# A half tile times its norm weight, made by ACT in place of DVE

## The chip, the cores and the metric

The kernel runs on one core of a Trainium2 chip. Five engines matter: PE (TensorE, the matrix products), DVE (VectorE), ACT (ScalarE), POOL (GpSimd, used here almost only to issue transfers) and SP (SyncE, which issues the other transfers). Each engine works through its own list of instructions in order and meets the others only at semaphores. The metric is the time of one execution in microseconds; the figure for the kernel before is the median of three runs, 1158.26 us.

## The reference

A small decoder trunk: 512 tokens, width 1024, two layers. The first mixes by a gated delta rule, the second by sliding-window attention; both also attend to 256 memory tokens. Behind the mixing, each layer has a gated feed forward of width 2816. Cut to what matters here:

```python
def swiglu(h, w_gate_up, w_down):
    gu = h @ w_gate_up
    return (jax.nn.silu(gu[..., :D_FF]) * gu[..., D_FF:]) @ w_down

for layer in range(DEPTH):
    ...
    x = x + concatenate([mix_out, mem_o], -1) @ w_out[layer]
    x = x + swiglu(rms_norm(x, ln_ffn[layer]), w_gate_up[layer], w_down[layer])
```

`rms_norm(x, g)` divides each token by its root mean square and multiplies each of the 1024 features by its weight g.

## The kernel before, in words

Activations stand with features on the 128 partitions and the 512 tokens along the free axis, so x is eight tiles of 128x512. The root mean square is divided out after the products (`rstd`); what goes into them is h = x times g. Every fp32 operand is split in two: a rounded high part, written by ACT (`copy`, line 138: an activation of kind Copy, with an optional scale per partition), and the rest, written by DVE. A product is then three matmuls: high by high, high by low, low by high (`mm3`). `weight` (line 181) splits a loaded weight tile in this way into whi and wlo; `split_gain` (line 171) does the same for x times g.

**The output projection** (`output`, line 933) runs over eight rows m. When PE has finished row m, DVE adds it to the residual x[m] (the last of these additions is kept as `self.ended`), ACT makes the high part of h[m], DVE the low part l, ACT squares x[m] (sq) and DVE adds the square to a running sum (sqa). One matmul with ones over that sum gives `rstd`.

**The feed forward** (`ffn`, line 966) begins with gate 0 and up 0, then gates 1 and 2, all as plain products of 512 tokens. From then on gate and up columns are made in pairs by `quarters` (line 1109), which splits weights and tokens in halves and forms seven products of half size in place of eight, as Strassen's scheme does. A pair adds weight halves on DVE and on POOL's queue (accumulating transfers into the ws tiles), splits each sum, and copies intermediate results out of PSUM on ACT (the fs tiles) before PE adds the next product onto the same bank.

**The token sums** (`token_sums`, line 1082) are the other operand of these products: combinations of the two token halves of x[j] and x[j + 4], each times its weight. There are four of them per layer (j = 0 to 3), each made once and used by all later products. For one j, the code makes

- c: the second half of x[j] times its weight, 128x256 (one buffer, so the next j must wait for its readers)
- t0: the first half of x[j] times its weight, less c; t1 from t0 and x[j + 4]; t2: the second half of x[j + 4] times its weight, less c; t3 from t1. All four are quarters of one tile, raw
- the split of raw into two T tiles, high on ACT and low on DVE

c is read by t0 and t2.

**What sets the order.** The program is traced in the order of the code; a planner then puts each engine's instructions into a list of its own, by its own estimates of when each can start, in which instructions from later in the code may move up into gaps. It places the token sums among the last rows of the output projection, gate 0 and up 0. Where its choice is not wanted, the code adds an edge without a semaphore (`nosync`) that keeps two instructions of one engine in order. In the second layer such an edge keeps c of j = 1 to 3 behind `self.ended`, the last residual addition.

Of the kernel before, what the change touches and what calls it, by code (L numbers as in the profile page):

```python
# [13 lines left out]
ALU = mybir.AluOpType  # L14
# [71 lines left out]
class Builder:  # L86
# [995 lines left out]
    def token_sums(self, fp, layer, j, h):  # L1082


        nc, q = self.nc, T // 2
        if j == 0:
            self.minus = self.t(fp, [P, 4], F32, "minus")
            self.ts(self.minus, self.gains[:, G_FFN[layer] + 4:G_FFN[layer] + 8], -1.0, ALU.mult)
        g0, g1 = (self.gain(G_FFN[layer], j + i) for i in (0, 4))
        n1 = self.minus[:, j:j + 1]  # L1090
        x0, x1 = self.x[j], self.x[j + 4]
        c = self.t(fp, [P, q], F32, "fc")
        raw = self.t(fp, [P, D], F32, "raw")
        t = [raw[:, i * q:(i + 1) * q] for i in range(4)]
        ins = nc.vector.tensor_scalar(out=c, in0=x0[:, q:], scalar1=g0, scalar2=None, op0=ALU.mult).ins
        if layer and j:

            self.nosync(ins, self.ended)
        self.stt(t[0], x0[:, :q], g0, c, ALU.mult, ALU.subtract)
        self.stt(t[1], x1[:, q:], n1, t[0], ALU.mult, ALU.subtract)  # L1100
        self.stt(t[2], x1[:, q:], g1, c, ALU.mult, ALU.subtract)
        self.stt(t[3], x1[:, :q], n1, t[1], ALU.mult, ALU.subtract)
        hl = self.weight(None, raw=raw, pool=fp, tags=("T", "T"), bufs=8)
        parts = {f"t{i + 1}": [x[:, i * q:(i + 1) * q] for x in hl] for i in range(4)}
        parts["11"] = [x[:, :q] for x in h[j]]
        parts["21"], parts["22"] = ([x[:, i * q:(i + 1) * q] for x in h[j + 4]] for i in range(2))
        return parts
# [304 lines left out]
```

## Time and profile before

| what | value |
|---|---|
| median of three runs | 1158.26 us (1158.03 to 1158.34) |
| the profiled execution's own time | 1158.37 us |
| its span, first to last instruction | 1156.6 us |
| busy: PE, DVE, ACT | 1138.6, 834.8, 627.3 us |
| the changed line, L1095: instructions, median | 8, 0.346 us |
| where it runs | 308.2 us (first layer) to 812.9 us (second layer) |

In the lists below, a row gives the start in us from the span's start, the length in us, the engine, the line of the kernel, the operation, and what it writes and reads with partitions x elements; x2 at the end means two in a row, whose length is their sum. In brackets stands the time the engine was idle before it, and what ended that. Lengths include a tail in which the next instruction has already begun, so the step from start to start is what an instruction takes from a full list. Lines of waits read: engine, tile and line that waited, who was waited for: us in total, times, longest.

### The profile page before, as it was taken

The page shows a single profiled execution, that of the slowest core. Times are in us where ns is not written, and L with a number is a line of the kernel's source. Part 1 is how long each engine was busy: PE and PEld are TensorE (multiplying, and loading weights), DVE is VectorE, ACT ScalarE, POOL GpSimd, SP SyncE. Part 2 cuts the span into 40 slices and gives each one's busy share as a digit, 9 for nine tenths or more (in the row PEclk, how much of TensorE's full clock was granted, in tenths as well). Part 3 has the DMA queues.
Part 4 walks back from the last instruction along what each step waited for, and adds up shares of the span by engine and source line. Part 5 has one row for each costly group of instructions (what it writes and reads, how often), then busy time and mean ns, then how long its engine had stood idle before and what let it go on. Part 6 is the DMA issues. An engine that isn't in the chain of part 4 may idle for free.

```text
span 1156.6 us, 19275 instructions
## 1 busy us (share of the span) xinstructions
PE 1138.6 (98%) x7330; PEld 995.3 (86%) x7330; DVE 834.8 (72%) x1559; ACT 627.3 (54%) x1251; POOL 85.1 (7%) x97
## 2 busy tenths in 40 slices
PE   7999999999999999999999999999999999999996
PEld 7788777877899998899998877788899988999986
DVE  5674886767888877488965777839988644889554
ACT  6489572366566642256653554856666412666433
POOL 0220000000101101011100000001011000111000
PEclk9999999999999999999999999999999999999999
DMA  8243441225657736367623421116577633676232
GB/s 311 85 150 110 135 120 65 91 92 164 183 130 176 177 103 167 114 168 178 161 84 97 124 73 40 53 55 197 130 177 188 155 92 111 169 188 151 78 98 84
DMA packets 72559, 151.20 MB, mean 131 GB/s; under 512 B 16732, under 2 KB 18932, under 8 KB 72468
## 3 DMA queue, kind: packets, MB, share of 16 engines
q1 hardware_dynamic: 61332, 129.54, 35.8%
q0 software_dynamic: 11136, 20.45, 11.1%
q8 instruction: 57, 0.93, 0.3%
q14 instruction: 34, 0.28, 0.1%
HBM read 143.00 MB, written 6.96 MB: 130 GB/s over the span
## 4 chain that ended last, share of the span: by engine, by line
PE 93%; DVE 4%; ACT 1%; DMA 1%; issue 0%; DVEq 0%; SPq 0%; ACTq 0%
PE pj L145 43%; PE g L145 38%; PE sc L145 6%; PE qk L145 3%; PE pt L145 2%; PE pt L149 1%; DVE wlo L152 1%; ACT sm L133 1%; DVE qv L155 1%; DVE big L152 0%; PE g L149 0%; DVE kn L155 0%; DVE btmp L152 0%; DMA wraw<-in_win 0%; DMA mem<-in_memT 0%
## 5 line engine op out<-in xcount | busy, mean ns | idle before, releaser
L139 ACT ACTIVATE whi<-wraw 128x512 fp32r<-128x512 f32 (+3 forms) x324 | 241.0, 750 | 254.6 <-PE pj L145 155.1
L152 DVE TENSOR_TENSOR wlo<-wraw,whi 128x512 fp32r<-128x512 f32 (+3 forms) x324 | 271.2, 846 | 100.5 <-ACT whi L139 94.3
L145 PE MATMUL pj<-h,whi 128*128 128x512 f32 (+1 forms) x652 | 257.4, 396 | 0.0
L145 PE MATMUL pj<-l,whi 128*128 128x512 f32 (+1 forms) x652 | 255.0, 392 | 0.0
L145 PE MATMUL pj<-h,wlo 128*128 128x512 f32 (+1 forms) x652 | 254.2, 391 | 0.0
L145 PE MATMUL g<-T,whi 128*128 128x256 f32 x1216 | 220.6, 282 | 0.9 <-ACT fs L139 0.9
L145 PEld LDWEIGHTS g<-T,whi 128*128 128x128 f32 x1216 | 187.0, 189 | 2.2 <-DVE fu L155 1.1
L145 PE MATMUL g<-T,wlo 128*128 128x256 f32 x608 | 171.1, 281 | 0.0
L145 PEld LDWEIGHTS pj<-h,whi 128*128 128x128 f32 x652 | 122.5, 188 | 28.6 <-issue 3.6
L145 PE MATMUL g<-h,whi 128*128 128x256 f32 (+1 forms) x500 | 146.6, 293 | 0.0
L145 PE MATMUL g<-h,wlo 128*128 128x256 f32 (+1 forms) x500 | 145.8, 292 | 0.0
L145 PE MATMUL g<-l,whi 128*128 128x256 f32 (+1 forms) x500 | 145.5, 291 | 0.0
L145 PEld LDWEIGHTS pj<-l,whi 128*128 128x128 f32 x652 | 122.6, 188 | 25.3 <-issue 1.1
L145 PEld LDWEIGHTS pj<-h,wlo 128*128 128x128 f32 x652 | 122.6, 188 | 25.3 <-issue 0.6
L145 PEld LDWEIGHTS g<-T,wlo 128*128 128x128 f32 x608 | 114.4, 188 | 0.0
L145 PEld LDWEIGHTS g<-h,whi 128*128 128x128 f32 x500 | 95.0, 190 | 2.3 <-issue 0.5
L145 PEld LDWEIGHTS g<-l,whi 128*128 128x128 f32 x500 | 94.9, 190 | 2.3 <-issue 0.5
L145 PEld LDWEIGHTS g<-h,wlo 128*128 128x128 f32 x500 | 95.0, 190 | 1.7
L1120 POOL DMA_DIRECT2D ws<-in_wgu x38 | 33.6, 884 | 722.7 <-ACT h L139 231.8
L139 ACT ACTIVATE whi<-ws 128x512 fp32r<-128x512 f32 x76 | 47.9, 631 | 49.2 <-PE g L145 41.4
L152 DVE TENSOR_TENSOR fu<-pj,rstd 128x512 f32<-128x512 f32 (+1 forms) x34 | 22.4, 659 | 54.4 <-PE pj L145 54.4
L152 DVE TENSOR_TENSOR wlo<-ws,whi 128x512 fp32r<-128x512 f32 x76 | 52.0, 685 | 7.5 <-ACT whi L139 7.3
(379 smaller groups left out, 1695.2 us busy)
## 6 DMA issues: line engine op xcount, KB each, us to landing
wraw<-in_wgu SPq DMA_DIRECT2D x50, 512.0 KB, 4.3
ws<-in_wgu SPq DMA_DIRECT2D x76, 256.0 KB, 3.6
ws<-in_wgu POOLq DMA_DIRECT2D x76, 256.0 KB, 4.8
wraw<-in_win SPq DMA_DIRECT2D x26, 512.0 KB, 3.5
wraw<-in_wdn SPq DMA_DIRECT2D x32, 384.0 KB, 3.1
wraw<-in_wdn SPq DMA_DIRECT2D x32, 320.0 KB, 2.9
wraw<-in_wgu SPq DMA_DIRECT2D x38, 256.0 KB, 4.3
wraw<-in_wout SPq DMA_DIRECT2D x16, 512.0 KB, 3.6
```

Of the source, the lines that this page charges most:

```text
L133: ins = self.nc.scalar.activation(out, in_, func, **kw).ins
L139: self.copied = self.nc.scalar.activation(out, in_, AF.Copy, **kw).ins
L145: return self.nc.tensor.matmul(out, lhsT, rhs, start=start, stop=stop, skip_group_check=more).ins
L149: return self.nc.tensor.transpose(out, in_, self.ident[:k, :k]).ins
L152: return eng.tensor_tensor(out=out, in0=a, in1=b, op=op).ins
L155: return self.nc.vector.scalar_tensor_tensor(out=out, in0=in0, scalar=scalar, in1=in1, op0=op0, op1=op1).ins
L1120: nc.gpsimd.dma_start(s1, a22, accum_op=ALU.add)
```

## The change

c is made by ACT's scaled copy in place of DVE's multiplication. The edge behind `self.ended`, which was put on c, is now put on t0, the next instruction of DVE.

```diff
         t = [raw[:, i * q:(i + 1) * q] for i in range(4)]
-        ins = nc.vector.tensor_scalar(out=c, in0=x0[:, q:], scalar1=g0, scalar2=None, op0=ALU.mult).ins
+        self.copy(c, x0[:, q:], scale=g0)
+        ins = self.stt(t[0], x0[:, :q], g0, c, ALU.mult, ALU.subtract)
         if layer and j:
 
             self.nosync(ins, self.ended)
-        self.stt(t[0], x0[:, :q], g0, c, ALU.mult, ALU.subtract)
         self.stt(t[1], x1[:, q:], n1, t[0], ALU.mult, ALU.subtract)
```

## The prediction

> **What bounds the kernel now.** I read the totals first, then the busy time by stretch, then who makes PE wait, and only then the lists of the three engines around the two places where the changed line runs.
>
> ```profile
> PE 1138.6 (98%) x7330; PEld 995.3 (86%) x7330; DVE 834.8 (72%) x1559; ACT 627.3 (54%) x1251; POOL 85.1 (7%) x97
> ...
> PE 93%; DVE 4%; ACT 1%; DMA 1%; issue 0%; DVEq 0%; SPq 0%; ACTq 0%
> ...
> L1095 DVE TENSOR_SCALAR fc<-x,gains x8: 344/346/349, 308.2 to 812.9; 128x256 f32<-128x256 f32 x8
> ...
> 308.00:334.00 26.00, 26.00 (x119) 21.36 (x119) 23.95 (x43) 14.93 (x21) 3.50 (x4) 1.00 0.65 168
> 812.00:826.00 14.00, 13.12 (x72) 11.24 (x71) 13.54 (x25) 8.92 (x16) 0.86 (x1) 1.00 0.24 58
> ...
> 660.00:788.00 128.00, 127.93 (x797) 99.98 (x796) 88.02 (x257) 79.77 (x222) 0.00 (x0) 1.00 0.21 67
> ```
>
> PE sets the time. In a stretch row the figures after the length are busy us of PE, PEld, DVE, ACT and POOL. In the first layer's token sums (308 to 334) PE has no gap; in the second layer's it misses 0.88 us between 812 and 826, where DVE is busy 13.54 of 14 us and ACT 8.92. The changed line runs eight times, four in each place. What PE waited for between 300 and 826, and what DVE waited for between 788 and 826:
>
> ```profile
> PE g L145 <- ACT fs L139: 0.9, 1, 0.9
> ...
> DVE l L155 <- ACT h L139: 2.0, 1, 2.0
> DVE wlo L152 <- ACT whi L139: 0.4, 2, 0.3
> ```
>
> So one wait, for one ACT instruction, is all that PE loses near the change. Its history, from the lists of ACT, DVE and PE (start, length):
>
> ```profile
> 822.20 0.69 DVE L152 TENSOR_TENSOR wraw<-wraw 128x512 f32<-128x512 f32 x1
> 822.98 0.63 ACT L139 ACTIVATE whi<-wraw 128x512 fp32r<-128x512 f32 x1 [1.84 <-DVE wraw L152]
> ...
> 824.56 0.61 ACT L139 ACTIVATE whi<-wraw 128x512 fp32r<-128x512 f32 x1
> 825.08 0.36 ACT L139 ACTIVATE fs<-g 128x256 f32<-128x256 f32 x1
> 825.49 0.50 PE L145 MATMUL g<-T,whi 128*128 128x256 f32 x2 [0.88 <-ACT fs L139]
> ```
>
> ACT stood idle 1.84 us for DVE's add of two weight halves, then ran without a gap (two more instructions between the rows shown), and fs is the fifth; PE may add the next product to that bank only when fs has copied it. DVE's lateness at 822.20 is therefore paid by PE, one for one, up to 0.88 us.
>
> **The change, part by part.** Removed from DVE: eight multiplications. Added to ACT: eight scaled copies of the same half tile. New waits: DVE's first product of a token sum (t0) waits for ACT; and, as the tile c has one buffer, ACT's next c waits for DVE's third product (t2) of the sum before. No transfer is added or moved, so the SP queue keeps its list; POOL's queue, which waits for readers of the ws buffers, can only see DVE readers a little earlier.
>
> What leaves DVE is the step from the start of c to the start of the next instruction:
>
> ```profile
> 798.24 0.34 DVE L1095 TENSOR_SCALAR fc<-x,gains 128x256 f32<-128x256 f32 x1
> 798.62 0.48 DVE L155 SCALAR_TENSOR_TENSOR raw<-x,gains,fc 128x256 f32<-128x256 f32 x1
> 799.02 0.68 DVE L152 TENSOR_TENSOR x<-pj,x 128x512 f32<-128x512 f32 x1
> ...
> 802.87 0.75 DVE L155 SCALAR_TENSOR_TENSOR l<-x,gains,h 128x512 fp32r<-128x512 f32 x1 [1.98 <-ACT h L139]
> 803.53 0.69 DVE L152 TENSOR_TENSOR sqa<-sqa,sq 128x512 f32<-128x512 f32 x1
> ...
> 805.48 0.35 DVE L1095 TENSOR_SCALAR fc<-x,gains 128x256 f32<-128x256 f32 x1
> 805.74 1.22 DVE L152 TENSOR_TENSOR wlo<-wraw,whi 128x1024 fp32r<-128x1024 f32 x1
> ...
> 811.67 0.87 DVE L155 SCALAR_TENSOR_TENSOR raw<-x,gains,fc 128x256 f32<-128x256 f32 x2
> ...
> 812.86 0.35 DVE L1095 TENSOR_SCALAR fc<-x,gains 128x256 f32<-128x256 f32 x1
> 813.12 0.48 DVE L155 SCALAR_TENSOR_TENSOR raw<-x,minus,raw 128x256 f32<-128x256 f32 x1
> ...
> 816.47 0.88 DVE L155 SCALAR_TENSOR_TENSOR raw<-x,gains,fc 128x256 f32<-128x256 f32 x2
> ```
>
> In the second layer the first c (0.38 us of step) lies ahead of DVE's 1.98 us wait for h: it frees nothing, that wait just grows. The three later ones (first and last shown) step 0.26 us each, and behind 802.87 DVE waits only the 0.4 us of the row above. So 3 x 0.26 = 0.78 us goes from a full list, the add at 822.20 starts at 821.42, fs ends 0.78 earlier, and of PE's 0.88 us some 0.1 is left: **-0.78 us**. Late next is PE's own arrival.
>
> What ACT gets, by the nearest rows (the same shape and scale operand, at the end of the kernel), and the places where it can lie:
>
> ```profile
> L139 ACT ACTIVATE T<-x,gains x12: 494/495/497, 1131.2 to 1136.1; 128x256 f32<-128x256 f32 x12
> ...
> 1132.12 4.49 ACT L139 ACTIVATE T<-x,gains 128x256 f32<-128x256 f32 x11
> ...
> 796.52 0.61 ACT L142 ACTIVATE sq<-x 128x512 f32<-128x512 f32 x1
> 801.16 1.06 ACT L139 ACTIVATE whi<-wraw 128x1024 fp32r<-128x1024 f32 x1 [4.03 <-DMA wraw<-in_wgu]
> 802.13 0.71 ACT L139 ACTIVATE h<-x,gains 128x512 fp32r<-128x512 f32 x1
> ...
> 808.84 1.06 ACT L139 ACTIVATE T<-raw 128x1024 fp32r<-128x1024 f32 x1 [2.71 <-DVE raw L155]
> 818.77 1.06 ACT L139 ACTIVATE T<-raw 128x1024 fp32r<-128x1024 f32 x1 [2.01 <-DVE raw L155]
> ```
>
> One takes 0.495 us, and in a row 4.49 / 11 = 0.41. ACT's gaps of 4.03, 2.71, 2.01 and 1.84 us hold one each, and c's input was complete rows earlier, so I cost the copies at nothing on the path. If that cover is missing, a copy pushes what stands behind it by 0.41. Where exactly the planner places them no row shows. Bounds: from below the whole 0.88 of PE's wait goes (-0.88); from above the copy lands behind the whi that waits 4.03 us, which is the third rival. I take -0.78, since c(0) fits in the 4.03 gap and a later c has time: both readers of the third c (the pair at 811.67) are done by 812.54, and the fourth is first read at 816.47, 3.9 us on.
>
> First layer: DVE there has room, and PE does not wait.
>
> ```profile
> 332.93 0.69 DVE L152 TENSOR_TENSOR fg<-pj,rstd 128x512 f32<-128x512 f32 x1 [1.33 <-PE pj L145]
> ```
>
> DVE catches up with PE and idles 1.33 us before the products begin, so 0.26 us less, four times, makes that idle longer: **0**. The moved ordering edge costs nothing by itself: it keeps t0 of the later sums behind the last residual add, as it kept c.
>
> Sum: -0.78 us. The profiled execution took 1158.37 us in all (span 1156.6, 1.77 around it), so 1157.59 on its own base; that execution lies 0.11 above the median of 1158.26, so 1157.5 as a median. A change within 0.2% (2.3 us, 1155.9 to 1160.6) is about what a measurement of this kernel cannot tell from none.
>
> **The rivals.** First, *nothing moves*: something else ends fs late, for instance a different ACT order in front of it. Then 1158.3. For it: fs already stands behind four ACT instructions it does not need. Against: all four are back to back, and the one idle ahead of them is put down to DVE.
>
> Second, *the hand-over is exposed*: t0 waits for a copy that ACT begins only when t0 is next. DVE then pays 0.495 plus the 0.03 between the end of h (802.13 + 0.71) and l at 802.87, less the 0.26 saved, three times: +0.8, which fs and PE follow: 1159.1. Against: those 3.9 us. [...]
>
> Third, on the other side, *c(0) behind a waiting weight*: the planner lists ACT's c(0) after the whi that waits (for a transfer in the second layer, for PE in the first), and keeps t0 ahead of the last residual add x on DVE. It has already put that whi ahead of an h that was ready sooner. The rows for the first layer and for PE:
>
> ```profile
> 310.03 0.47 DVE L155 SCALAR_TENSOR_TENSOR raw<-x,minus,raw 128x256 f32<-128x256 f32 x1
> 310.43 0.68 DVE L152 TENSOR_TENSOR x<-g,x 128x512 f32<-128x512 f32 x1
> 314.14 0.69 DVE L152 TENSOR_TENSOR sqa<-sqa,sq 128x512 f32<-128x512 f32 x1
> ...
> 310.10 1.06 ACT L139 ACTIVATE whi<-wraw 128x1024 fp32r<-128x1024 f32 x1 [3.29 <-issue]
> 311.07 1.05 ACT L139 ACTIVATE T<-raw 128x1024 fp32r<-128x1024 f32 x1
> ...
> 315.53 1.02 PE L145 MATMUL g<-sqa,consts 128*128 128x512 f32 x2
> ...
> 804.28 1.12 PE L145 MATMUL g<-sqa,consts 128*128 128x512 f32 x2
> ```
>
> Second layer: c(0) at 802.13 to 802.63, t0 one step of 0.4 us, x at 803.06 to 803.75, h 0.71 more, l at 804.46 against 802.87: 1.6 later with one product ahead of x, 2.8 with four. PE's sum of squares (804.28) has 0.06 us to spare behind sqa, so PE is 1.5 to 2.7 late there; fs is late by that less the 0.78 saved: +0.7 to +1.9. First layer: c(0) ends at 311.56 behind whi, and x moves from 310.43 to 312.0 (one product ahead) or 313.2 (four), 1.6 or 2.8 late; sqa has 0.7 to spare (314.83 against 315.53): +0.9 to +2.1. In today's lists one product stands ahead of x in the second layer and four in the first, which gives 0.7 + 2.1 = +2.8 and 1161.1; the ends are 1159.9 and 1162.3. It decides as slower from both layers together on. Against: ACT is idle 4.03 and 3.29 us before these two whi, with c's input ready.
>
> *Faster by over 0.2%* would need 2.3 us of PE waits, and there are 0.88 around the change; the 128 us of attention behind the first layer hold 0.07. Only a reordering elsewhere would do it.
>
> **How the numbers follow.** The forecast 1157.5 has 0.46, with a range of its own of 1157.2 to 1158.0; nothing moves 0.09; exposed hand-over 0.12; the waiting weight 0.26, of which 0.03 stays under 1160.6; faster by a reordering 0.07. So within 0.2%: 0.46 + 0.09 + 0.12 + 0.03 = 0.70; slower 0.23; faster 0.07. The range runs from 1157.0 (all of PE's wait gone, and 0.2 of spread) to 1161.8, most of the third rival; left out are the faster case and that rival's upper end.
>
> **What would show it.** Right: c rows on ACT of about 0.495 us, c(0) ahead of the whi near 801; DVE's list from l to wraw 0.78 us shorter; PE's wait for fs at 0.1 us; no new PE wait near 315 and 804. Wrong: DVE rows t0 released by ACT c, an x add later than 799 or 310.4 against PE's rows, or PE waiting for h, l or sqa. A PE or transfer list in another order than before, far from the two places, would break the argument altogether.

## The result, and the profile after

The changed kernel takes 1160.53 us in the median (1159.02 to 1164.06) against 1158.28 us before (1157.39 to 1158.87) in the same comparison: a ratio of 1.0021, interval 1.0013 to 1.0028. It is slower by 2.25 us, where 0.8 us less had been forecast. The profiled execution took 1159.56 us with a span of 1157.8, which is 1.19 us over the profiled execution of before; the rest of the difference of the medians is the subject of the last section. One execution of the kernel before (2891.29 us) and one of the changed kernel (1732.60 us) are far off all others and are left out of every figure.

In the first layer nothing is lost. Between 788 and 840 us, around the token sums of the second layer, PE loses 1.11 us more than before (51.12 less 50.01). The busy time by stretch, first of the kernel after, then of the kernel before (after the length stand PE, PEld, DVE, ACT and POOL, then the granted clock):

```profile
308.00:334.00 26.00, 26.00 (x122) 21.48 (x121) 23.19 (x38) 16.71 (x25) 3.50 (x4) 1.00 0.61 163
...
788.00:840.00 52.00, 50.01 (x281) 43.01 (x280) 45.24 (x75) 32.44 (x53) 6.93 (x8) 1.00 0.58 157
```

```profile
788.00:840.00 52.00, 51.12 (x293) 44.54 (x292) 47.93 (x81) 31.85 (x51) 6.94 (x8) 1.00 0.60 163
```

In place of one wait PE now has three, and DVE waits longer and for other things. What PE waited for between 280 and 840 us, and DVE between 785 and 835, in the kernel after:

```profile
PE g L145 <- ACT fs L139: 1.0, 1, 1.0
PE g L145 <- DVE T L152: 0.6, 1, 0.6
PE pj L145 <- DVE l L155: 0.4, 1, 0.4
...
DVE T L152 <- ACT T L139: 3.3, 2, 2.2
DVE wlo L152 <- ACT whi L139: 2.8, 3, 2.3
```

The lists of PE, SP and POOL are the same as before, instruction by instruction. Those of DVE and ACT are not: in the first layer some T moved, and in the second the planner put the lists together anew. DVE's list after, from the low part of gate 1's weight on:

```profile
801.82 1.23 DVE L152 TENSOR_TENSOR wlo<-wraw,whi 128x1024 fp32r<-128x1024 f32 x1 [2.33 <-ACT whi L139]
802.97 0.75 DVE L155 SCALAR_TENSOR_TENSOR l<-x,gains,h 128x512 fp32r<-128x512 f32 x1
...
805.83 1.23 DVE L152 TENSOR_TENSOR T<-raw,T 128x1024 fp32r<-128x1024 f32 x1 [1.12 <-ACT T L139]
...
812.75 1.23 DVE L152 TENSOR_TENSOR T<-raw,T 128x1024 fp32r<-128x1024 f32 x1 [2.20 <-ACT T L139]
...
823.14 0.69 DVE L152 TENSOR_TENSOR wraw<-wraw 128x512 f32<-128x512 f32 x1
823.75 1.22 DVE L152 TENSOR_TENSOR T<-raw,T 128x1024 fp32r<-128x1024 f32 x1
```

ACT's list after:

```profile
800.73 1.06 ACT L139 ACTIVATE whi<-wraw 128x1024 fp32r<-128x1024 f32 x1 [4.23 <-DMA wraw<-in_wgu]
801.69 0.49 ACT L139 ACTIVATE fc<-x,gains 128x256 f32<-128x256 f32 x1
802.09 0.71 ACT L139 ACTIVATE h<-x,gains 128x512 fp32r<-128x512 f32 x1
...
808.07 0.51 ACT L139 ACTIVATE fc<-x,gains 128x256 f32<-128x256 f32 x1 [1.32 <-DVE raw L155]
808.49 0.67 ACT L133 ACTIVATE rstd<-g,eps 128x512 f32<-128x512 f32 x1
809.19 0.63 ACT L133 ACTIVATE rstd<-rstd 128x512 f32<-128x512 f32 x1
809.84 1.28 ACT L124 ACT_TABLE_LOAD   x1
811.13 0.63 ACT L133 ACTIVATE fg<-fg 128x512 f32<-128x512 f32 x1
811.67 1.04 ACT L139 ACTIVATE T<-raw 128x1024 fp32r<-128x1024 f32 x1
```

Three things are new in them. The low part wlo of gate 1's weight, which needs a transfer and ACT's whi, stands ahead of l of the last row; before, it stood 2.87 us behind l (805.74 against 802.87). On ACT, T of the second token sum stands behind both rstd, the table load and the silu of gate 1, where before it stood ahead of the second rstd; DVE waits 2.20 us for it. And the low T of the last token sum stands behind the add wraw, where before it stood ahead of it (820.46 against 822.20), so PE meets it late. ACT also stands 1.32 us at the c of 808.07, until DVE has read the c before it. The rows of before for the second and third of these places, first ACT's second rstd (its T stood at 808.84), then DVE's low T:

```profile
809.81 0.61 ACT L133 ACTIVATE rstd<-rstd 128x512 f32<-128x512 f32 x1
...
820.46 1.22 DVE L152 TENSOR_TENSOR T<-raw,T 128x1024 fp32r<-128x1024 f32 x1
```

From l of the last row to the add wraw, DVE's list now takes 823.14 - 802.97 = 20.17 us, where before it took 822.20 - 802.87 = 19.33: 0.84 longer, where 0.78 shorter had been forecast. PE's rows after:

```profile
803.76 0.50 PE L145 MATMUL pj<-l,whi 128*128 128x512 f32 x1 [0.41 <-DVE l L155]
...
825.02 0.38 PE L145 MATMUL g<-T,whi 128*128 128x256 f32 x1 [0.55 <-DVE T L152]
...
826.55 0.50 PE L145 MATMUL g<-T,whi 128*128 128x256 f32 x2 [1.03 <-ACT fs L139]
```

The copies themselves are as forecast: eight of 493 to 511 ns.

### The profile page after: what moved, and what is told of

The parts are those of the page before. It is cut to its first block, busy times and chain, and to the rows that moved or that the text cites. A ratio compares the mean times of both kernels' runs of the same rounds, so it can differ in the third digit from the quotient of the medians.

```text
span 1157.8 us, 19274 instructions
## 1 busy us (share of the span) xinstructions
PE 1138.8 (98%) x7330; PEld 994.4 (86%) x7330; DVE 832.1 (72%) x1551; ACT 631.4 (55%) x1259; POOL 86.0 (7%) x97
## 4 chain that ended last, share of the span: by engine, by line
PE 90%; DVE 5%; ACT 2%; DMA 1%; issue 1%; SPq 0%; DVEq 0%; ACTq 0%
PE pj L145 42%; PE g L145 37%; PE sc L145 6%; PE qk L145 3%; PE pt L145 1%; PE pt L149 1%; DVE wlo L152 1%; PE g L149 1%; DMA wraw<-in_wgu 1%; DMA wraw<-in_wmk 1%; ACT sm L133 1%; DVE qv L155 1%; DVE big L152 0%; DVE T L152 0%; DVE btmp L152 0%
```

## The experiments

Each kernel was timed against the kernel before on the same chip. The table gives the median of each less the median of before in its comparison; the intervals are about 1.0 us to either side.

| kernel | us | less before | ratio (interval) |
|---|---|---|---|
| changed kernel | 1160.53 | +2.25 | 1.0021 (1.0013 to 1.0028) |
| first_layer_only | 1158.39 | -0.19 | 0.9996 (0.9987 to 1.0005) |
| second_layer_only | 1160.13 | +1.55 | 1.0014 (1.0005 to 1.0023) |
| low_part_behind_l | 1159.51 | +0.93 | 1.0007 (0.9999 to 1.0016) |
| c_behind_square | 1160.34 | +1.85 | 1.0018 (1.0010 to 1.0027) |
| both_pins | 1159.18 | +0.69 | 1.0005 (0.9996 to 1.0014) |
| own_places | 1159.85 | +1.28 | 1.0011 (1.0002 to 1.0020) |
| both_pins_own_places | 1158.71 | +0.14 | 1.0001 (0.9992 to 1.0010) |
| own_places_t_behind | 1158.24 | -0.42 | 0.9997 (0.9988 to 1.0006) |
| fewer_c | 1158.76 | +0.19 | 1.0002 (0.9993 to 1.0010) |
| fewer_c_t_behind | 1158.38 | -0.28 | 0.9998 (0.9989 to 1.0006) |
| before_l_behind_low_part | 1159.91 | +1.42 | 1.0013 (1.0004 to 1.0023) |
| h_before_weight | 1157.30 | -1.28 | 0.9987 (0.9979 to 0.9996) |
| before_h_before_weight | 1156.98 | -1.51 | 0.9988 (0.9979 to 0.9997) |

**Which layer.** The change in one layer alone; the other keeps DVE's multiplication and its edge.

```diff
-        self.copy(c, x0[:, q:], scale=g0)
+        if not layer:                      # second_layer_only: if layer
+            self.copy(c, x0[:, q:], scale=g0)
+        else:
+            ins = nc.vector.tensor_scalar(out=c, in0=x0[:, q:], scalar1=g0, scalar2=None, op0=ALU.mult).ins
```

> c on ACT in the first layer alone, the second layer as before. Theory (the loss is made by the lists of the second layer, where the low part of gate 1's weight now stands ahead of l of the last row, and c of j=1 ahead of h): no loss, 1158.3 within 0.5 us, with the narrow spread of the kernel before. Rival (the copies and the hand-over from ACT to DVE cost wherever they are): half of the 2.25 us, 1159.4.

> c on ACT in the second layer alone. Theory: the whole loss and the wide spread, 1160.5. Rival (hand-over everywhere): half of it, 1159.4.

The first layer gives no difference that can be measured, the second alone is slower by 1.55 us. The loss is in the layer whose lists were put together anew.

**The low part of the weight ahead of l.** In the changed kernel an edge puts wlo of gate 1's weight back behind l of the last row; and the other way round, in the kernel before, with c on DVE, an edge puts l behind that wlo.

```diff
+    if layer and i == 0:
+        self.nosync(self.wlow, self.l7)    # low_part_behind_l: wlo waits for its turn behind l
+        self.nosync(self.l7, self.wlow)    # before_l_behind_low_part: l behind wlo
```

> The changed kernel with one edge more, without a semaphore: on DVE the low part of gate 1's weight (wlo) stays behind l of the last row in the second layer; c is on ACT in both layers as in the changed kernel. Theory: DVE no longer waits for the weight's transfer ahead of l, most of the loss goes: 1158.5 to 1159.2 (c of j=1 still stands ahead of h, 0.41 us). Rival (hand-over): nothing changes, 1160.5.

> The kernel before (c on DVE) with one edge: in the second layer l of the last row stays behind the low part of gate 1's weight (wlo), as it came out in the changed kernel. The planner then also puts sqa ahead of wlo. Theory (the place of wlo costs by itself, whoever makes c): sqa waits for sq until 803.4, wlo to 804.6, l at 804.5 in place of 802.87, so PE waits 1.5 us for l near 804; DVE's list is only 0.5 late behind it, the 0.88 us wait for fs goes, and the end moves by +0.6, to about 1159.1. Rival (the loss needs c on ACT): no change, 1158.4.

The first takes 1.0 to 1.3 us off the changed kernel's loss (+0.93, for +2.25 and, in a later comparison, +1.89). Not all of that is this one place: with the edge the planner put much of both lists back, the low T of the last token sum too, which stands ahead of wraw again. The second is the cleaner test, as it moves only l, sqa, one c and this wlo. It makes the kernel before 1.42 us slower with c left on DVE, so this order is a loss by itself, whoever makes c. The eleven executions fall into two groups: six took 1159.14 to 1159.91 us, 0.7 to 1.4 over the kernel before, where 0.6 was expected, and five took 1160.97 to 1161.34, at a mean granted clock of 0.996 to 0.997, where five of the six had 0.998 (last section). PE waits there for l; in the execution shown, one of the slower five, the wait was long:

```profile
806.20 0.50 PE L145 MATMUL pj<-l,whi 128*128 128x512 f32 x1 [2.41 <-DVE l L155]
```

**ACT's c ahead of h.** c of the later sums is put behind the last row's square on ACT, so that the c at 801.69 no longer stands between whi and h.

```diff
         self.copy(c, x0[:, q:], scale=g0)
+        if layer and j:
+            self.nosync(self.copied, self.squared)
```

> The changed kernel with c of j = 1 to 3 on ACT behind the last square in the second layer; it only moves c of j=1 from ahead of h to behind sq, DVE's list is the changed kernel's. Theory (wlo ahead of l binds): h is 0.41 us earlier, but l still waits for wlo, so 1160.2 to 1160.5. Rival (the 0.41 us of c ahead of h is the loss): 0.4 to 0.8 less, 1159.8.

It stays at +1.85, and DVE's list from l to wraw at 20.17 us (803.10 to 823.27): the 0.41 us by which that c holds up h is not the loss as long as wlo stands ahead of l.

**Both orders as before.** The two edits together restore the order around the last row.

> The changed kernel with both: wlo behind l on DVE, and c of j=1 behind the last square on ACT. This is the order of the kernel before around the last row, with c on ACT. Theory: PE's 0.3 us wait for l goes, the wait for fs shrinks; if the sum of the prediction holds once the order is kept, 1157.6 to 1158.0; if the later copies of c (in front of whi and rstd) still delay DVE, 1158.4 to 1159.0.

+0.69, better than either alone but not the forecast -0.8. The trace shows the next cause, c's single buffer. ACT's c of the third sum waits until DVE has read the second's, and the weight's whi stands behind it on ACT, so DVE waits for that whi. First ACT's rows, then DVE's, then PE's wait:

```profile
807.92 0.51 ACT L139 ACTIVATE fc<-x,gains 128x256 f32<-128x256 f32 x1 [2.87 <-DVE raw L155]
808.34 1.04 ACT L139 ACTIVATE whi<-wraw 128x1024 fp32r<-128x1024 f32 x1
...
809.42 1.23 DVE L152 TENSOR_TENSOR wlo<-wraw,whi 128x1024 fp32r<-128x1024 f32 x1 [0.67 <-ACT whi L139]
...
PE g L145 <- ACT fs L139: 1.4, 1, 1.4
```

**A place for each c.** In the second layer the second to fourth c get places of their own, in tables (cosT and sinT) that are no longer read there.

```diff
-        c = self.t(fp, [P, q], F32, "fc")
+        own = {1: self.cosT[:, :q], 2: self.cosT[:, q:], 3: self.sinT[:, :q]} if layer else {}
+        c = own[j] if j in own else self.t(fp, [P, q], F32, "fc")
```

> The changed kernel with a place of its own for each of c(1), c(2) and c(3) in the second layer and nothing else. Theory (two causes side by side: the low part of the weight ahead of l, and ACT held up by c's one buffer): the first stays, so PE still waits some 0.4 for l near 804 and DVE about 2 for whi; the second goes; 1159.3 to 1160.0. Rival A (the one buffer is the whole loss): 1158.0. Rival B (it is no part of it): 1160.5, as the changed kernel.

> The changed kernel with both orders around the last row of tokens as before (low part behind l, c(1..3) behind the last square), and with a place of its own for each of c(1), c(2) and c(3) in the second layer (in tables that are no longer read there), so that ACT need not wait for DVE to have read the c before. Theory (ACT, standing at fc(2) for c's one buffer, 2.87 us, holds up the whi behind it and so DVE's wlo by 0.67): the waits of fc(2) and of wlo near 809 go, DVE's list gets the relief that was forecast, 1157.6 to 1158.3. Rival (the one buffer costs nothing that PE waits for): 1159.2 as with the two orders alone, PE's wait for fs stays near 1.4.

Alone it leaves +1.28, as the theory of two causes side by side had it; with both orders +0.14. The medians thus put ACT's standing at c's single buffer at 0.6 to 1.0 us and the orders at 1.1 to 1.6, but each of them has an interval of 1.0 us to either side. The traces agree in kind, with about half the size: between 788 and 840 us PE loses 1.99 us in the changed kernel, 1.60 with the places, 1.40 with the orders and 1.03 with both. PE's wait for fs is still 1.0 us with both, though, and three c are gone from DVE's list.

**Fewer c, with ACT left alone.** To see what three c steps are worth on DVE by themselves, the kernel before makes c once in a layer and uses it four times; three of the four sums are then not those of the reference, so this is for measuring only. The edge stands on t0, as in the changed kernel.

```diff
+        if j == 0:
+            self.c = self.t(fp, [P, q], F32, "fc")
+        c = self.c
...
+        if j == 0:
+            nc.vector.tensor_scalar(out=c, in0=x0[:, q:], scalar1=g0, scalar2=None, op0=ALU.mult)
```

> The kernel before with c made once in a layer instead of four times: the second to fourth token sums of a layer take the c of the first, so three multiplies of a half tile in each layer are left out and those sums are not what the reference has. ACT's list is that of before. If DVE's lateness is paid by PE one for one, as the prediction took it, three steps of 0.26 us out of DVE's list in the second layer give 1157.5 to 1157.9 and PE's wait for fs falls from 0.88 to some 0.1 to 0.3. Rival (DVE stands waiting somewhere behind them and gives the 0.78 back): 1158.4, the wait as before.

The rival came out: 1158.76, and PE waits as before. In its trace DVE's list from l to the add wraw is 823.43 - 803.92 = 19.51 us, where before it was 822.20 - 802.87 = 19.33: not 0.78 shorter but 0.18 longer.

```profile
PE g L145 <- ACT fs L139: 1.1, 1, 1.1
...
803.92 0.75 DVE L155 SCALAR_TENSOR_TENSOR l<-x,gains,h 128x512 fp32r<-128x512 f32 x1 [1.91 <-ACT h L139]
...
808.46 1.00 DVE L155 SCALAR_TENSOR_TENSOR raw<-x,minus,raw 128x256 f32<-128x256 f32 x2
809.37 1.22 DVE L152 TENSOR_TENSOR wlo<-wraw,whi 128x1024 fp32r<-128x1024 f32 x1
...
814.14 0.68 DVE L152 TENSOR_TENSOR fu<-g,fg 128x512 f32<-128x512 f32 x1
815.35 1.23 DVE L152 TENSOR_TENSOR T<-raw,T 128x1024 fp32r<-128x1024 f32 x1 [0.53 <-ACT T L139]
816.50 0.69 DVE L152 TENSOR_TENSOR wlo<-wraw,whi 128x512 fp32r<-128x512 f32 x1
...
823.43 0.69 DVE L152 TENSOR_TENSOR wraw<-wraw 128x512 f32<-128x512 f32 x1
```

The kernel before, at the same pair of products:

```profile
807.67 0.47 DVE L155 SCALAR_TENSOR_TENSOR raw<-x,minus,raw 128x256 f32<-128x256 f32 x1
808.07 0.34 DVE L1095 TENSOR_SCALAR fc<-x,gains 128x256 f32<-128x256 f32 x1
808.33 0.47 DVE L155 SCALAR_TENSOR_TENSOR raw<-x,minus,raw 128x256 f32<-128x256 f32 x1
808.73 1.22 DVE L152 TENSOR_TENSOR wlo<-wraw,whi 128x1024 fp32r<-128x1024 f32 x1
```

Two things take the gain. First, t3 reads t1. With c between them the three steps take 808.73 - 807.67 = 1.06 us; without it the two take 809.37 - 808.46 = 0.91, so a c that stands there is worth 0.15 and not 0.26. Of the three c, two stood there. Second, the planner now lists T of the third sum ahead of a half weight's low part. T waits 0.53 us for ACT's copy; before, that low part filled the time.

**That T put back.** The only difference from the kernel just shown, and from the one with places for each c, is that T of the third sum, on ACT and on DVE, again stands behind the half weight.

```diff
+        if layer and j == 2:
+            self.held_back = (self.copied, self.low)
...
             self.split(raw, *w)
+            if getattr(self, "held_back", None):
+                self.nosync(self.held_back[0], self.copied)
+                self.nosync(self.held_back[1], self.low)
+                self.held_back = None
```

> fewer_c (second to fourth token sums of a layer take the c of the first, so those sums are not what the reference has), with the third T of the second layer put behind the half weight on ACT and on DVE, as it stands in the kernel before: DVE's list in the second layer is then that of before without three fc rows and with nothing else changed. Theory (fewer_c gave 0.53 of its 0.78 back because that T came first and waited for ACT's copy): the wait of T for T near 815 goes, from l to the add wraw 18.9 to 19.0 us instead of 19.5 (19.3 before), PE's wait for fs 0.4 to 0.6, time 0.4 to 0.6 under fewer_c, 1158.0 to 1158.3. Rival (PE's wait near 826 is set by something that DVE's list does not move): wait 0.9 to 1.1, 1158.6 to 1158.8.

> both_pins_own_places with the third T of the second layer put behind the half weight on ACT and on DVE, as it stands in the kernel before: with c on ACT, every order of before is now restored, and no c waits for another's buffer. Theory: the wait of 0.53 at T goes, PE's wait for fs falls from 1.0 to some 0.5, 1158.0 to 1158.4. Rival: c on ACT holds the copies up elsewhere, wait 1.0, 1158.7.

The traces bear out the theory. With c left out, DVE's list in the second layer is now that of before less three rows:

```profile
PE g L145 <- ACT fs L139: 0.4, 1, 0.4
...
803.28 0.75 DVE L155 SCALAR_TENSOR_TENSOR l<-x,gains,h 128x512 fp32r<-128x512 f32 x1 [1.86 <-ACT h L139]
...
814.71 1.23 DVE L152 TENSOR_TENSOR T<-raw,T 128x1024 fp32r<-128x1024 f32 x1
...
822.18 0.68 DVE L152 TENSOR_TENSOR wraw<-wraw 128x512 f32<-128x512 f32 x1
```

From l to wraw it is 822.18 - 803.28 = 18.90 us, 0.43 under before, and PE's wait falls from 0.88 to 0.4: one for one in the trace; the median moves by -0.28, within its interval. With c on ACT and these orders restored (not all of them: T of the first sum stands behind wlo on DVE, and T of the second ahead of the first rstd on ACT) the list is 18.90 us as well (804.43 to 823.33), PE shows no wait, and the median is 0.42 us under before, which its interval of 1.0 us to either side does not tell from none. That no wait was left there is in part that execution's own: its l ran 2.07 us ahead of PE's sum of squares, against 1.41 before, and it is the slowest of its kernel's eleven (1159.64), at a mean granted clock of 0.997, where six of the eleven had 0.998.

```profile
804.43 0.75 DVE L155 SCALAR_TENSOR_TENSOR l<-x,gains,h 128x512 fp32r<-128x512 f32 x1 [1.57 <-ACT h L139]
...
806.50 1.02 PE L145 MATMUL g<-sqa,consts 128*128 128x512 f32 x2
...
823.33 0.68 DVE L152 TENSOR_TENSOR wraw<-wraw 128x512 f32<-128x512 f32 x1
```

**h ahead of the waiting weight.** What DVE's list is late for, in the kernel before too, is h behind the whi that waits 4 us for its transfer. One edge puts that whi behind h of the last row; in the changed kernel, and in the kernel before.

```diff
+    if layer and i == 0:
+        self.nosync(self.whigh, self.h7)
```

> The changed kernel with another edge: on ACT the high part of gate 1's weight (whi), which waits for its transfer, stays behind h of the last row in the second layer. Theory: neither ACT nor DVE waits for the transfer ahead of h and l, so PE's waits near 804 and 825 go: 1157.0 to 1158.0, spread no wider than before. Rival (hand-over): 1160.5, as c is still on ACT and DVE still waits for it.

> The kernel before (c on DVE) with the other edge: on ACT the high part of gate 1's weight stays behind h of the last row in the second layer. Theory (the transfer in front of h is what makes DVE late): DVE's 1.98 us wait for h goes, the wait for fs goes with it, 1157.4, the same as the changed kernel with this edge. Rival (c on ACT is what brought that kernel to 1157.3): 1158.4, no change.

1157.30 and 1156.98: 1.28 and 1.51 us under before, and PE has no wait left between 280 and 840 us in either. Of the kernel before with this edge, where l now starts 3.45 us ahead of PE's sum of squares:

```profile
788.00:840.00 52.00, 52.00 (x306) 46.00 (x306) 49.09 (x84) 32.72 (x52) 7.82 (x9) 1.00 0.62 165
...
800.03 0.75 DVE L155 SCALAR_TENSOR_TENSOR l<-x,gains,h 128x512 fp32r<-128x512 f32 x1
...
803.48 1.02 PE L145 MATMUL g<-sqa,consts 128*128 128x512 f32 x2
```

The gain is the edge's; with it, it makes no measurable difference which engine makes c. This version, with c left on DVE, is faster than both kernels. The gain is over the 0.88 us of PE's wait; the trace does not say where the other 0.6 are from, and they lie within the interval.

**The changed kernel again.** Three more profiled executions, for the clock (last section).

> The changed kernel once more, for a second profiled execution. If a granted clock of half for some 3 us behind PE's waits is what takes its slower executions beyond the profiled one, the windows behind 804 or 826 show a clock below 1.00 in an execution that is over 1160; with a clock of 1.00 throughout it should be 1159.0 to 1159.8.

> The changed kernel, one look. If half the granted clock behind PE's waits makes its slower executions, an execution over 1160.3 shows a stretch of some 3 us with a clock of 0.5 to 0.9 behind 804 or 826, and one under 1160 shows 1.00.

> The changed kernel, one more look, with the same expectation: clock 1.00 from 780 to 840 under 1160, below that behind a wait of PE above it.

They took 1159.27, 1160.51 and 1161.27 us, each with nearly the same waits of PE (1.6 to 2.1 us in sum between 788 and 840), and with a DVE list of 20.17 us from l to wraw. The second, over 1160.3 with a clock of 1.00 in every stretch up to 1086 us, goes against its expectation.

## Why the prediction was wrong

- **"DVE's lateness at 822.20 is paid by PE, one for one"**: right, in the trace. 0.43 us off DVE's list took 0.4 us off PE's wait (fewer_c_t_behind).
- **First layer 0, moved edge 0**: right. The first layer alone gives 1158.39 against 1158.58; the first two c (306.17 and 308.61 in the changed kernel) stood ahead of the whi that had waited (now at 310.43), as the forecast had it.
- **The term of -0.78 us**: wrong even on DVE alone. It was three steps of 0.26. Two of them stood between dependent products and were worth 0.15 and 0.14 (1.06 - 0.92 at the third sum), so 0.55 in all; the list shortened by 0.43, since fg came to wait for an rstd that stood behind a T on ACT. And that only with the list held: left to the planner, one T ahead of a low part gave the whole of it back.
- **"I cost the copies at nothing on the path"**: this is the step that failed. The prediction looked for gaps of ACT that hold 0.41 us, and there are such gaps. It took the lists as given, but for c, and said itself that no row shows where the planner puts the copies. What the copies cost is not their time. They brought other lists: the kernel that merely lacks three c on DVE kept nearly the old ones, and the one with c on ACT did not. In the new ones DVE's list from l to wraw is 0.84 us longer instead of 0.78 shorter, and PE waits 1.11 us more, with wlo ahead of l and T behind the table load. With c still on ACT but these orders held and a place for each c, the list is 18.90 us and no loss is left that can be measured (own_places_t_behind). Why the planner's estimates gave these lists the traces cannot tell. And where ACT comes to a c whose buffer DVE has not read, it stands waiting (1.32 us at 808.07 in the changed kernel, 2.87 in both_pins) with the rstd or the next weight's whi behind it; the prediction named this wait for t2 and costed it by the gap (3.9 us), not by what is queued behind it.
- **The third rival**, c(0) behind the waiting weight, had the right place in the second layer (the whi near 801, and l late for PE), but the wrong instruction. c(0) was made early, ahead of that whi, in both layers; it was gate 1's low part on DVE and a later c on ACT that came ahead of l and h. Its first half, the first layer, did not happen. That the measured time lies between this rival's ends (1159.9 to 1162.3) is luck, since 0.9 to 2.1 us of it was for a layer that lost nothing.
- **The second rival**, an exposed hand-over, had the right direction (1159.1) and the wrong mechanism: no row of t0 waits for ACT's c in the second layer. DVE waits for ACT's T and whi instead.
- **Engine time** did not decide: a copy on ACT takes 493 to 511 ns where DVE's multiplication took 344 to 349, but ACT never filled up (32.44 us busy of 52 after, 31.85 before), and with the orders held no difference between the two engines is left that can be measured (-0.42 us, own_places_t_behind).
- **What would show it wrong**: "PE waiting for h, l or sqa" came true at 803.76. The lists did change order, though not those of PE and of the transfers.
- **One slip in the working**, which decides nothing: all of PE's wait gone, with 0.2 of spread, gives 1157.2 and not 1157.0.

## What to carry to other kernels

Before costing an edit of one instruction, ask which list will be put together anew because of it: where a planner orders in-order engines, the instruction's time can be the smaller part, and what then stands behind a wait the larger. A hand-over from one engine to another through a single buffer makes the writer wait too, and everything queued behind it on that engine (1.32 us in the changed kernel, 2.87 in both_pins); give it a buffer, or count that queue. And before moving work off a late engine, look at what makes it late: here one edge, putting h ahead of a weight that waits for its transfer, brought more (1.28 and 1.51 us) than all of the moved work could (0.78 by the forecast).

## What was not expected of the hardware

In some executions the granted clock fell to a half after waits of PE of 1.6 or 2.4 us in sum. In the changed kernel's fourth profiled execution PE waited 0.54 and 1.04 us just before 826.73, and the matmuls of 128x256 that step 0.12 us then stepped 0.21 from 827.8 to 831.1 us. The clock stands behind POOL's column:

```profile
826.00:828.00 2.00, 1.27 (x9) 1.27 (x10) 1.68 (x4) 1.99 (x5) 0.00 (x0) 0.94 0.41 66
828.00:830.00 2.00, 2.00 (x11) 2.00 (x11) 1.85 (x3) 0.90 (x2) 0.00 (x0) 0.50 0.80 304
830.00:832.00 2.00, 2.00 (x14) 2.00 (x14) 0.57 (x3) 0.63 (x1) 0.67 (x1) 0.70 0.74 201
832.00:834.00 2.00, 2.00 (x19) 2.00 (x18) 1.78 (x4) 0.63 (x1) 1.06 (x2) 1.00 0.77 142
```

The first profiled execution, with the same waits (0.55 and 1.03), kept its clock:

```profile
828.00:830.00 2.00, 2.00 (x20) 2.00 (x19) 1.98 (x4) 1.27 (x3) 0.00 (x0) 1.00 0.78 292
```

It took 1159.56 us and the fourth 1161.27, 1.71 us more: some 3.4 us at half the clock lose 1.7. The same fall is in the execution shown of before_l_behind_low_part, after its 2.41 us wait (0.80, 0.50 and 0.85 in three stretches of 2 us from 806 to 812), and in that of c_behind_square, after waits of 0.54 and 1.03 us (0.90, 0.50 and 0.74 from 826 to 832). So it comes in some executions and not in others with the same lists.

What sets them apart no run was made to test; there is an estimate, from the clock's records and PE's rows. The record of the kernel before holds 1.00 for 1140.052 us from its first entry to its one change, at the end, that of the first execution after for 1143.465: they differ by 3.413 us and are 334 and 335 times that, and the falls are some 3.4 us long too. If the clock changes in steps of that length, then a step of the first execution, counted from its first entry at 9.93 us, ends at 825.72, within the second wait, with PE idle 0.75 us in the step up to there and 0.83 in the next. In the fourth, the 3.4 us up to the fall near 827.8 hold both waits, 1.58 us; in c_behind_square they hold 1.57 and in before_l_behind_low_part 2.41. It does not cover every loss of clock: both_pins_own_places has a mean of 0.996 with 1.00 in every stretch looked at from 596 to 1086 us, and where and why it lost the rest is not shown.

This is part of the 2.25 us: PE's additional waits account for 1.11, and a fall in some of the executions for some of the rest. For the executions without a profile only the mean granted clock is on record. Among the profiled ones it is 0.998 in after, both_pins and after_third, which show no such fall, and 0.997 both with one (after_fourth, c_behind_square) and without (before_h_before_weight). Of the changed kernel's thirteen, the three slowest (1161.80 to 1164.06 us) have 0.995 or 0.996, less than any of these, four (1159.31 to 1160.07) have 0.998, and six, with 0.997, cannot be told. It is not all, as the execution of 1160.51 us had none; in it the work around 804 already ran 1.06 us later than in the first (l at 804.03 against 802.97), and PE had already been busy 0.29 us less between 60 and 200 us (139.05 against 139.34), ahead of all that the change touches.
